# Weight transfers of 512 KB into six half-size buffers in a two-layer encoder kernel

## The chip, the cores and the metric

The kernel runs on one core of a Trainium2 chip. The metric is the device time of one execution in microseconds (us). Before the change the median of three runs is 2024.06 us (2023.92 to 2024.22).

## The reference, cut to what matters

The reference is two layers of an encoder over 256 tokens of width 2048, in float32:

```
h = RMSNorm(x);  [q | k | v | gu | gv] = h @ w_in
A = windowed attention on q, k, v (8 query heads, 2 key heads, a sink per head)
B = gelu(gu) * (W_s @ LayerNorm(gelu(gv)) + b_s)
x = x + concat(RMSNorm(A), RMSNorm(B)) @ w_o
x = x + (silu(g) * u) @ w_down,   [g | u] = DWConv3(RMSNorm(x) @ w_up)      # width 5632
```

Nearly all of the arithmetic is in the five products with weights. Each weight is read from memory once.

## The kernel before, in words

**Arithmetic.** TensorE (PE) multiplies in a reduced float32 form, so each operand is a sum of a rounded part, hi, and a rest, lo. A weight block is multiplied as hi against [hi | lo] of the activations (512 columns, L187 or L224), and as lo against the activations' hi (256 columns, L197 or L230). In the input projection of q, k, v and gv the activations stand still instead (L154 to L157). The products lo times lo are left out.

**How weights arrive.** `split_weights` takes 1024 KB of weights (128 partitions x 2048 numbers), which is eight blocks of 128 x 256. SP issues one transfer into a buffer called raw (L116; three buffers of 8 KB per partition). Then, for each half h of it (1024 numbers per partition), ScalarE (ACT) copies the half into a hi tile (L126) and VectorE (DVE) subtracts to get the lo tile (L108). There are four hi and four lo tiles. A raw buffer is free again when the lo of its second half is made; a lo tile is free again when the last lo matmul that reads it is done. The last transfer of a group of w_down holds four blocks, so 512 KB. In `pair`, which runs two weight columns of w_up together, the lo parts of the second column are made later (`split_later`).

**The order of work.** Each engine runs its instructions in a fixed order. That order is made at build time by a scheduler which places an instruction when its operands and buffers would be ready; code under `urgent()` gets a high priority, and `split_weights` is such code. The number, size and grouping of buffers therefore moves instructions of all engines, and the line order of the program doesn't tell where.

**The end of the first half of a layer.** The change and the prediction touch this stretch most. `gated(u)` computes a piece of gu (unit, L187 and L197), `spatial(u)` the product with W_s (L608), `gate(u)` multiplies both on DVE (L632) and adds its squares to a sum (ACT L276, DVE L277). There are four such pieces. `inv_rms_cols` then turns a sum of squares into 1/rms: DVE adds both halves of the sum (L289), PE sums over the partitions (L291), DVE scales (L281: `av` for attention, `sv` for gating), and GpSimd (POOL) takes the power (L283: `ar`, `sr`). `as_rows` spreads the result over partitions with two PE transposes (L298) and an ACT copy into rb (L300). `normed` then makes eight pairs of activation tiles for w_o: for each tile, DVE scales (L456), ACT makes hi (L254), DVE makes lo (L255).

**What covers the wait.** The product with w_o needs the attention half first. Three output columns are begun with it (`pre`, three units of L187 and L197 on attention tiles), and only then is each finished with the gating half:

```
663  pre = [unit(atts, w_o[l, u], None, 0, NK // 2, last=False) for u in range(3)]
666          ps = unit(mixT, w_o[l, u], pre[u], NK // 2, NK, first=False)
```

While PE works on `pre`, the chain from the last gate through L289, L291, L281, L283, L298, L300, L456, L254 has to be finished.

The product with w_up, `pair`, runs 32 hi matmuls of one column, 32 of the other, and then the 64 lo matmuls of both; it comes 21 times in each layer.

Of the kernel before, what the change touches and what calls it, by code (L numbers as in the profile page):

```python
# [8 lines left out]
F32 = mybir.dt.float32  # L9
# [5 lines left out]
P = 128  # L15
# [10 lines left out]
W = 512  # L26
KB = 4
# [13 lines left out]
def encoder(ctx: ExitStack, tc: tile.TileContext, xT, w_in, w_gu, w_o, w_up, w_down, wsT, pcol, prow, rope, out):  # L41
    nc = tc.nc
    pool = lambda name, bufs, **kw: ctx.enter_context(tc.tile_pool(name=name, bufs=bufs, **kw))
# [2 lines left out]
    slots = pool("slots", 42)  # L46
    rowp = pool("rowp", 4)
    evp = pool("evp", 4)
    rawp = pool("rawp", 3)
    hip = pool("hip", 4)  # L50
    lop = pool("lop", 4)
    scr = pool("scr", 4)
# [22 lines left out]
    def tp(shape):  # L75
        return tpp.tile(shape, F32, tag="tp", name="tp")

    xs = [const.tile([P, 2, SEQ], F32, tag=f"xs{j}", name=f"xs{j}") for j in range(NK // 2)]

    def urgent():  # L80
        return tc.high_priority(offset=AHEAD)


    def load_first(dst, src):
        tc.keep_in_program_order(nc.sync.dma_start(dst, src))
# [5 lines left out]
    with urgent():  # L91
        nc.vector.memset(ones, 1.0)

        warm = tp([P, P])
        for _ in range(WARM):
            nc.tensor.matmul(warm, ones, ones, start=True, stop=True)
        first_raws = [rawp.tile([P, 4 * W], F32, tag="raw", name="raw") for _ in range(2)]
        for k in range(KB):
            load_first(xs[k // 2][:, k % 2, :], xT[:, k, :])
            load_first(first_raws[0][:, k * W : (k + 1) * W], w_in[0, 2, :, k * W : (k + 1) * W])  # L100
        for k in range(KB):
            load_first(first_raws[1][:, k * W : (k + 1) * W], w_in[0, 0, :, k * W : (k + 1) * W])
    mhalf = const.tile([P, 8], F32, tag="mhalf", name="mhalf")
    nc.scalar.activation(mhalf, ones[:, :8], AF.Copy, scale=-0.5)

# [1 line left out]
    def lo_part(lo, part, hi):  # L107
        nc.vector.tensor_tensor(out=lo, in0=part, in1=hi.bitcast(F32), op=ALU.subtract)  # L108

    def split_weights(src, loaded=None, later=None):  # L110
        n = src.shape[-1]
        with urgent():
            raw = loaded
            if raw is None:
                raw = rawp.tile([P, 4 * W], F32, tag="raw", name="raw")
                nc.sync.dma_start(raw[:, :n], src)  # L116

            step = 2 * W if loaded is None else W
            his, los = [], []
            for h in range(0, n, 2 * W):  # L120
                hi = hip.tile([P, 2 * W], F32R, tag="hi", name="hi")
                lo = lop.tile([P, 2 * W], F32R, tag="lo", name="lo") if later is None else None
                for a in range(0, 2 * W, step):
                    part = raw[:, h + a : h + a + step]
                    cs = slice(a, a + step)
                    nc.scalar.activation(hi[:, cs], part, AF.Copy)  # L126
                    if later is None:
                        lo_part(lo[:, cs], part, hi[:, cs])
                    else:
                        later.append((part, hi[:, cs]))  # L130
                his.append(hi)
                los.append(lo)
        return his, los
# [12 lines left out]
    def rows_by_cols(ps, acts, src, first, last, raw=None):  # L146
        his, los = split_weights(src, raw)
        for kk in range(KB):
            cs = slice(kk % 2 * W, (kk % 2 + 1) * W)
            wh, wl = his[kk // 2][:, cs], los[kk // 2][:, cs]  # L150
            ms = [slice(m * P, (m + 1) * P) for m in range(2)]
            s0, s1 = first and kk == 0, last and kk == KB - 1
            for m in range(2):
                nc.tensor.matmul(ps[:, m, :], acts[kk][:, 0, ms[m]], wh, start=s0, stop=False)  # L154
                nc.tensor.matmul(ps[:, m, :], acts[kk][:, 1, ms[m]], wh, start=False, stop=False)  # L155
            for m in range(2):
                nc.tensor.matmul(ps[:, m, :], acts[kk][:, 0, ms[m]], wl, start=False, stop=s1)  # L157
# [5 lines left out]
    def unit(acts, w, ps=None, k0=0, k1=None, first=True, last=True):  # L163
# [3 lines left out]
        for g in range(k0, k1, 2 * UB):  # L167
            ks = range(g, min(g + 2 * UB, k1))
            his, los = [], []
            for b in range(g, ks.stop, UB):  # L170
                h, lo = split_weights(w[:, b * UW : min(b + UB, ks.stop) * UW])
                his += h
                los += lo
# [38 lines left out]
    def pair(acts, ws):  # L212
        pss, his, los, later = [mm(), mm()], [], [], []
        for n, w in enumerate(ws):
            hs = []
            for b in range(0, len(acts), UB):
                h, lo = split_weights(w[:, b * UW : (b + UB) * UW], later=later if n else None)
                hs += h
                los += lo if n == 0 else []
            for k in range(len(acts)):  # L220
                for i in range(2):
                    c = k % KB * UW + i * P
                    x1 = acts[k].rearrange("p a b -> p (a b)")
                    nc.tensor.matmul(pss[n][:, i, :], hs[k // KB][:, c : c + P], x1, start=k == 0, stop=False)  # L224
        for n in range(2):
            los = split_later(later) if n else los
            for k in range(len(acts)):
                for i in range(2):
                    c = k % KB * UW + i * P
                    nc.tensor.matmul(  # L230
                        pss[n][:, i, :SEQ], los[k // KB][:, c : c + P], acts[k][:, 0, :], start=False, stop=k == len(acts) - 1
                    )
        after_lo[0] = True
        return pss
# [111 lines left out]
    def rotate(rows, m, nh, tab):  # L346
        v = rows.rearrange("p (h d) -> p h d", d=HD)
        a = sl([P, nh, HD])
        nc.vector.tensor_tensor(
            out=a, in0=v, in1=tab[:, 0, m, :].unsqueeze(1).to_broadcast([P, nh, HD]), op=ALU.mult  # L350
        )
        b = sl([P, nh, HD])
        for lo, hi in ((0, 64), (64, 0)):
            nc.vector.tensor_tensor(
                out=b[:, :, lo : lo + 64],
                in0=v[:, :, hi : hi + 64],
                in1=tab[:, 1, m, lo : lo + 64].unsqueeze(1).to_broadcast([P, nh, 64]),
                op=ALU.mult,
            )
        nc.vector.tensor_tensor(out=a, in0=a, in1=b, op=ALU.add)  # L360
        return a
# [137 lines left out]
    for l in range(DEPTH):  # L499
# [38 lines left out]
        for m in range(2):  # L538
            a = rotate(kv[m][:, : 2 * HD], m, 2, tabs[1])
# [148 lines left out]
        for f0, f1 in ((0, 24), (24, NF)):  # L688
# [21 lines left out]
            for u in range(8):  # L710
                ps = [tp([P, W]) for _ in range(2)] if last and not more and u == 7 else mm()
                unit(ys, w_down[l, u, :, f0 * UW : f1 * UW], ps)
                if last and not more:
                    for i in range(2):
                        part = ps[i] if isinstance(ps, list) else ps[:, i, :]
# [64 lines left out]
```

## Time and profile before

| | |
|---|---|
| median of 3 runs | 2024.06 us |
| the profiled execution's own time | 2021.3 us |
| its span, first to last instruction | 2019.5 us |
| granted TensorE clock, mean | 1.000 |
| DVE busy | 1407.3 us (70%) |
| ACT busy | 1057.9 us (52%) |
| share of the 16 DMA engines taken by queue q1 (weights) | 53.6% |
| instructions of PE (matmuls) | 11324 |

A row of the timeline gives the start, the length, the engine, the line and operation, the tile written and the tiles read, the shape, and how many equal instructions in sequence it stands for; in square brackets stands the idle time before it and what ended that. The length of a PE row runs to the modelled end of its last matmul, so the rate of matmuls is read from start to start.

### The profile page before, as it was taken

The page shows a single profiled execution, that of the slowest core. Times are in us where ns is not written, and L with a number is a line of the kernel's source. Part 1 is how long each engine was busy: PE and PEld are TensorE (multiplying, and loading weights), DVE is VectorE, ACT ScalarE, POOL GpSimd, SP SyncE. Part 2 cuts the span into 40 slices and gives each one's busy share as a digit, 9 for nine tenths or more (in the row PEclk, how much of TensorE's full clock was granted, in tenths as well). Part 3 has the DMA queues.
Part 4 walks back from the last instruction along what each step waited for, and adds up shares of the span by engine and source line. Part 5 has one row for each costly group of instructions (what it writes and reads, how often), then busy time and mean ns, then how long its engine had stood idle before and what let it go on. Part 6 is the DMA issues. An engine that isn't in the chain of part 4 may idle for free.

```text
span 2019.5 us, 28222 instructions
## 1 busy us (share of the span) xinstructions
PE 2009.2 (99%) x11324; PEld 1761.7 (87%) x11324; DVE 1407.3 (70%) x1969; ACT 1057.9 (52%) x1429; POOL 20.7 (1%) x25
## 2 busy tenths in 40 slices
PE   9999999999999999999999999999999999999999
PEld 7888888898888888888888888889888888888888
DVE  6869767777755577777667797667777555777754
ACT  6575545555533355555445655555555334555542
POOL 0000000000000000000000000000000000000000
PEclk9999999999999999999999999999999999999999
DMA  8644555455555554555565345545555554455564
GB/s 292 224 148 150 179 175 203 171 174 213 197 188 188 189 186 167 204 201 189 182 245 183 130 167 171 205 167 175 210 199 202 190 188 171 167 205 210 177 212 136
DMA packets 59891, 380.25 MB, mean 188 GB/s; under 512 B 6896, under 2 KB 9968, under 8 KB 15984
## 3 DMA queue, kind: packets, MB, share of 16 engines
q1 hardware_dynamic: 59616, 378.43, 53.6%
q8 instruction: 88, 1.44, 0.3%
q14 instruction: 43, 0.35, 0.1%
q10 hardware_dynamic: 144, 0.02, 0.0%
HBM read 376.33 MB, written 2.10 MB: 187 GB/s over the span
## 4 chain that ended last, share of the span: by engine, by line
PE 98%; DVE 1%; POOL 0%; DMA 0%; ACT 0%; SPq 0%; issue 0%; DVEq 0%
PE mm L224 30%; PE mm L187 25%; PE mm L230 16%; PE mm L197 13%; PE mm L154 3%; PE mm L157 3%; PE mm L155 3%; PE tp L187 0%; PE tp L266 0%; PE tp L608 0%; PE tp L267 0%; PE tp L268 0%; PE tp L436 0%; DMA raw<-in_w_in 0%; PE tp L197 0%; DVE sl L261 0%
## 5 line engine op out<-in xcount | busy, mean ns | idle before, releaser
L108 DVE TENSOR_TENSOR lo<-raw,hi 128x1024 fp32r<-128x1024 f32 (+1 forms) x708 | 831.4, 1214 | 414.2 <-issue 137.8
L126 ACT ACTIVATE hi<-raw 128x1024 fp32r<-128x1024 f32 (+1 forms) x708 | 731.1, 1051 | 700.0 <-PE mm L187 319.2
L224 PE MATMUL mm<-sl,hi 128*128 128x512 f32 x2688 | 617.4, 389 | 0.0
L224 PEld LDWEIGHTS mm<-sl,hi 128*128 128x128 f32 x2688 | 501.9, 188 | 102.7
L187 PE MATMUL mm<-sl,hi 128*128 128x512 f32 x2264 | 529.4, 390 | 0.0
L187 PEld LDWEIGHTS mm<-sl,hi 128*128 128x128 f32 x2264 | 419.9, 188 | 83.6
L230 PEld LDWEIGHTS mm<-sl,lo 128*128 128x128 f32 x2688 | 328.1, 192 | 3.3
L230 PE MATMUL mm<-sl,lo 128*128 128x256 f32 x2688 | 329.1, 283 | 0.0
L197 PEld LDWEIGHTS mm<-sl,lo 128*128 128x128 f32 x2264 | 282.2, 191 | 7.6 <-ACT sl L254 1.9
L197 PE MATMUL mm<-sl,lo 128*128 128x256 f32 x2264 | 287.5, 284 | 0.0
L680 DVE SCALAR_TENSOR_TENSOR sc<-ev,pc,sc 128x255 f32<-128x255 f32 x176 | 81.0, 482 | 105.5 <-ACT sc L679 105.5
L154 PE MATMUL mm<-hi,sl 128*128 128x512 f32 x320 | 126.2, 394 | 0.1
L155 PE MATMUL mm<-hi,sl 128*128 128x512 f32 x320 | 125.2, 391 | 0.0
L239 ACT COPY ev<-mm 128x512 f32<-128x512 f32 x96 | 55.6, 579 | 129.5 <-PE mm L230 114.3
L157 PE MATMUL mm<-lo,sl 128*128 128x512 f32 x320 | 99.8, 391 | 0.0
L679 ACT ACTIVATE sc<-ev,pc 128x256 f32<-128x256 f32 x176 | 98.7, 586 | 0.0
L683 DVE SCALAR_TENSOR_TENSOR sc<-ev,pc,sc 128x255 f32<-128x255 f32 x176 | 80.9, 482 | 3.0
L154 PEld LDWEIGHTS mm<-hi,sl 128*128 128x128 f32 x320 | 60.3, 188 | 12.6 <-ACT hi L126 0.6
L155 PEld LDWEIGHTS mm<-hi,sl 128*128 128x128 f32 x320 | 60.1, 188 | 11.6
L157 PEld LDWEIGHTS mm<-lo,sl 128*128 128x128 f32 x320 | 59.7, 188 | 12.0
L254 ACT ACTIVATE sl<-sl 128x256 fp32r<-128x256 f32 x88 | 32.1, 409 | 71.3 <-DVE sl L701 71.3
L241 DVE TENSOR_TENSOR ev<-mm,ev 128x512 f32<-128x512 f32 x96 | 65.6, 684 | 0.0
(124 smaller groups left out, 787.9 us busy)
## 6 DMA issues: line engine op xcount, KB each, us to landing
raw<-in_w_up SPq DMA_DIRECT2D x176, 1024.0 KB, 6.0
raw<-in_w_down SPq DMA_DIRECT2D x80, 1024.0 KB, 5.1
raw<-in_w_in SPq DMA_DIRECT2D x38, 1024.0 KB, 5.0
raw<-in_w_o SPq DMA_DIRECT2D x32, 1024.0 KB, 5.1
raw<-in_w_gu SPq DMA_DIRECT2D x16, 1024.0 KB, 5.1
raw<-in_w_down SPq DMA_DIRECT2D x16, 512.0 KB, 3.6
sl<-in_prow SPq DMA_DIRECT2D x12, 256.0 KB, 6.1
raw<-in_w_in SPq DMA_DIRECT2D x8, 256.0 KB, 5.3
```

Source lines behind the costliest of these rows:

```text
L108: nc.vector.tensor_tensor(out=lo, in0=part, in1=hi.bitcast(F32), op=ALU.subtract)
L126: nc.scalar.activation(hi[:, cs], part, AF.Copy)
L154: nc.tensor.matmul(ps[:, m, :], acts[kk][:, 0, ms[m]], wh, start=s0, stop=False)
L155: nc.tensor.matmul(ps[:, m, :], acts[kk][:, 1, ms[m]], wh, start=False, stop=False)
L157: nc.tensor.matmul(ps[:, m, :], acts[kk][:, 0, ms[m]], wl, start=False, stop=s1)
L187: nc.tensor.matmul(bank[i], tile_of(his, k, i), x1, start=begins and k == k0, stop=flipped and tail and k == k1 - 1,)
L197: nc.tensor.matmul(bank[i][:, :SEQ], tile_of(los, k, i), acts[k][:, 0, :], start=False, stop=not flipped and tail and k == k1 - 1,)
L224: nc.tensor.matmul(pss[n][:, i, :], hs[k // KB][:, c : c + P], x1, start=k == 0, stop=False)
L230: nc.tensor.matmul(pss[n][:, i, :SEQ], los[k // KB][:, c : c + P], acts[k][:, 0, :], start=False, stop=k == len(acts) - 1)
L679: nc.scalar.activation(t[:, i, :], s[:, i, :], AF.Identity, bias=col(3), scale=col(1))
L680: nc.vector.scalar_tensor_tensor(out=t[:, i, 1:], in0=s[:, i, : SEQ - 1], scalar=col(0), in1=t[:, i, 1:], op0=ALU.mult, op1=ALU.add)
L683: nc.vector.scalar_tensor_tensor(out=t[:, i, : SEQ - 1], in0=s[:, i, 1:], scalar=col(2), in1=t[:, i, : SEQ - 1], op0=ALU.mult, op1=ALU.add)
```

## The change

The raw buffers become six of half the size, and the transfer moves into the loop over halves. So each half of 512 KB has its own buffer, its own transfer, its own hi and its own lo. The two transfers at the start of the program that come in pieces of 256 KB keep these pieces, but lie in two half buffers each. `split_weights` had 342 transfers of 1024 KB and now issues 684 of 512 KB for them; the 16 of 512 KB stay. The lines after L100 move: line 116 is line 119 now, and from the hi copy on each line is one higher (L126 is L127, L187 is L188, L291 is L292), while L108 keeps its number.

```diff
-    rawp = pool("rawp", 3)
+    rawp = pool("rawp", 6)
...
-        first_raws = [rawp.tile([P, 4 * W], F32, tag="raw", name="raw") for _ in range(2)]
-        for k in range(KB):
-            load_first(xs[k // 2][:, k % 2, :], xT[:, k, :])
-            load_first(first_raws[0][:, k * W : (k + 1) * W], w_in[0, 2, :, k * W : (k + 1) * W])
-        for k in range(KB):
-            load_first(first_raws[1][:, k * W : (k + 1) * W], w_in[0, 0, :, k * W : (k + 1) * W])
+        first_raws = [[rawp.tile([P, 2 * W], F32, tag="raw", name="raw") for _ in range(2)] for _ in range(2)]
+        for c, raws in zip((2, 0), first_raws):
+            for k in range(KB):
+                if c == 2:
+                    load_first(xs[k // 2][:, k % 2, :], xT[:, k, :])
+                load_first(raws[k // 2][:, k % 2 * W : (k % 2 + 1) * W], w_in[0, c, :, k * W : (k + 1) * W])
...
-            raw = loaded
-            if raw is None:
-                raw = rawp.tile([P, 4 * W], F32, tag="raw", name="raw")
-                nc.sync.dma_start(raw[:, :n], src)
 
             step = 2 * W if loaded is None else W
             his, los = [], []
             for h in range(0, n, 2 * W):
+                if loaded is None:
+                    raw = rawp.tile([P, 2 * W], F32, tag="raw", name="raw")
+                    nc.sync.dma_start(raw, src[:, h : h + 2 * W])
+                else:
+                    raw = loaded[h // (2 * W)]
...
-                    part = raw[:, h + a : h + a + step]
+                    part = raw[:, a : a + step]
```

The work of PE and DVE is the same, instruction for instruction; ACT has two more loads of its function table in layer 0. What moves is the order. In the feed-forward half of a layer the orders of PE agree but for small exchanges. In layer 0's attention two more halves are split ahead, and this shifts what follows.

PE in layer 0, at the sum of squares of the gating half. `tp_1863` is the sum over partitions, `sr_1869` its inverse root, `mm_2002` the third column of `pre`, whose hi matmuls are going on. Before:

```order
L187 MATMUL mm_2002<-sl_1522,hi_2009 128x512 x2
L187 MATMUL mm_2002<-sl_1527,hi_2009 128x512 x2
L291 MATMUL tp_1863<-ones_101,sl_1382 128x1 [waits DVE_49]
L291 MATMUL tp_1863<-ones_101,sl_1382 128x1
L187 MATMUL mm_2002<-sl_1532,hi_2009 128x512 x2
L298 MATMUL tp_1871<-ident_130,sr_1869 128x128 [waits Pool_49]
L298 MATMUL tp_1871<-ident_130,sr_1869 128x128
L187 MATMUL mm_2002<-sl_1537,hi_2009 128x512 x2
L197 MATMUL mm_2002<-sl_1502,lo_2006 128x256 x2
L197 MATMUL mm_2002<-sl_1507,lo_2006 128x256 x2
L197 MATMUL mm_2002<-sl_1512,lo_2006 128x256 x2
```

The same place after the change; `mm_2060` is the third column of `pre`, `sl_1932` to `sl_1967` are the tiles of the gating half:

```order
L198 MATMUL mm_2060<-sl_1559,lo_2064 128x256 x2
L198 MATMUL mm_2060<-sl_1564,lo_2070 128x256 [waits DVE_49]
L198 MATMUL mm_2060<-sl_1564,lo_2070 128x256
L198 MATMUL mm_2060<-sl_1569,lo_2070 128x256 x2
L198 MATMUL mm_2060<-sl_1574,lo_2070 128x256 x2
L198 MATMUL mm_2060<-sl_1579,lo_2070 128x256 x2
L292 MATMUL tp_1917<-ones_101,sl_1420 128x1 [waits DVE_49,PE_49]
L292 MATMUL tp_1917<-ones_101,sl_1420 128x1
L299 MATMUL tp_1925<-ident_132,sr_1923 128x128 [waits PE_49,Pool_49]
L299 MATMUL tp_1925<-ident_132,sr_1923 128x128
L198 MATMUL mm_1970<-sl_1932,lo_2108 128x256 [waits Activation_49]
...
L198 MATMUL mm_1970<-sl_1937,lo_2108 128x256 [waits Activation_49]
```

Four L187 of the third column and its 16 L197 stood behind L291 and around L298; now all of the third column stands ahead of L292, and the next matmul after the transposes reads a tile of the gating half.

DVE at the same place, up to the scaling `sv`. `sl_1382` is the sum of squares, a `lo` named here is for w_o, `sc_1859` the last piece of squares. Before:

```order
L277 TENSOR_TENSOR sl_1382<-sl_1382,sc_1763 128x512 [waits Activation_49]
L108 TENSOR_TENSOR lo_2048<-raw_2045,hi_2047 128x1024 [waits DMAHW6_49,PE_49]
L277 TENSOR_TENSOR sl_1382<-sl_1382,sc_1859 128x512 [waits DVE_49,Activation_49]
L108 TENSOR_TENSOR lo_2052<-raw_2045,hi_2051 128x1024 [waits PE_49]
L289 TENSOR_TENSOR sl_1382<-sl_1382 128x256 [waits DVE_49]
L281 TENSOR_SCALAR sv_1867<-tp_1863 128x2 [waits PE_49]
```

After; `sl_1420` is the sum, and with four lo tiles `lo_2161` takes the place of `lo_2064` and `lo_2167` that of `lo_2070`, the two that PE reads just ahead of L292:

```order
L108 TENSOR_TENSOR lo_2161<-raw_2158,hi_2160 128x1024 [waits DMAHW5_49,PE_49]
L278 TENSOR_TENSOR sl_1420<-sl_1420,sc_1813 128x512 [waits Activation_49]
L108 TENSOR_TENSOR lo_2167<-raw_2164,hi_2166 128x1024 [waits DMAHW6_49,PE_49]
L278 TENSOR_TENSOR sl_1420<-sl_1420,sc_1913 128x512 [waits DVE_49,Activation_49]
L290 TENSOR_TENSOR sl_1420<-sl_1420 128x256 [waits DVE_49]
L282 TENSOR_SCALAR sv_1921<-tp_1917 128x2 [waits PE_49]
```

Both additions to the sum now stand behind a lo that waits for PE. Before, `lo_2048` and `lo_2052` took the places of the lo tiles of the second column of `pre`, a whole run of hi matmuls earlier on PE.

ACT after the copy into rb, in the program after the change, where the tiles of the gating half get their hi (before, all eight stood in a row with no weight copy between them):

```order
L301 COPY rb_1928<-tp_1925 128x256 [waits PE_49]
L255 ACTIVATE sl_1932<-sc_1930 128x256 [waits DVE_49]
L255 ACTIVATE sl_1937<-sc_1935 128x256 [waits DVE_49]
L255 ACTIVATE sl_1942<-sc_1940 128x256 [waits DVE_49]
L255 ACTIVATE sl_1947<-sc_1945 128x256 [waits DVE_49]
L255 ACTIVATE sl_1952<-sc_1950 128x256 [waits DVE_49]
L255 ACTIVATE sl_1957<-sc_1955 128x256 [waits DVE_49]
L127 ACTIVATE hi_2215<-raw_2213 128x1024 [waits DMAHW7_49,PE_49,Activation_49]
L255 ACTIVATE sl_1962<-sc_1960 128x256 [waits DVE_49]
```

A hi copy, which itself waits for PE, has moved in ahead of the seventh tile.

## Rows read from the trace of the kernel before

**Rows 1.** The page, busy time by engine and the chain that ended last

```profile
PE 2009.2 (99%) x11324; PEld 1761.7 (87%) x11324; DVE 1407.3 (70%) x1969; ACT 1057.9 (52%) x1429; POOL 20.7 (1%) x25
PE 98%; DVE 1%; POOL 0%; DMA 0%; ACT 0%; SPq 0%; issue 0%; DVEq 0%
```

**Rows 2.** Waits of PE over the span: us in total, times, longest

```profile
PE tp L551 <- DVE sl L540: 1.0, 1, 1.0
PE tp L298 <- POOL sr L283: 0.9, 2, 0.4
PE tp L266 <- DVE sl L261: 0.6, 2, 0.4
PE tp L298 <- POOL ar L283: 0.5, 1, 0.5
```

**Rows 3.** Busy time by stretch, one in the feed-forward of layer 0

```profile
300.00:1000.00 700.00, 699.99 (x4032) 619.82 (x4032) 482.83 (x631) 360.21 (x470) 0.00 (x0) 1.00 0.54 190
```

**Rows 4.** Timeline of the feed-forward stage, one `pair` and the next

```profile
500.39 14.70 PE L224 MATMUL mm<-sl,hi 128*128 128x512 f32 x64
...
501.67 2.01 ACT L126 ACTIVATE hi<-raw 128x1024 fp32r<-128x1024 f32 x2 [0.49 <-DMA raw<-in_w_up]
...
514.92 7.83 PE L230 MATMUL mm<-sl,lo 128*128 128x256 f32 x64
...
522.59 14.70 PE L224 MATMUL mm<-sl,hi 128*128 128x512 f32 x64
```

**Rows 5.** Waits of SP over the span: us in total, times, longest

```profile
SPq L116 <- DVE lo L108: 1774.9, 346, 15.1
```

**Rows 6.** The page, weights' queue (packets, MB, share) and DMA issues (KB, us)

```profile
q1 hardware_dynamic: 59616, 378.43, 53.6%
...
raw<-in_w_up SPq DMA_DIRECT2D x176, 1024.0 KB, 6.0
...
raw<-in_w_down SPq DMA_DIRECT2D x16, 512.0 KB, 3.6
```

**Rows 7.** Timeline, DVE ahead of the gating sum in layer 0

```profile
197.45 1.22 DVE L108 TENSOR_TENSOR lo<-raw,hi 128x1024 fp32r<-128x1024 f32 x1
...
198.59 0.69 DVE L277 TENSOR_TENSOR sl<-sl,sc 128x512 f32<-128x512 f32 x1
...
199.19 1.22 DVE L108 TENSOR_TENSOR lo<-raw,hi 128x1024 fp32r<-128x1024 f32 x1
...
200.33 0.41 DVE L289 TENSOR_TENSOR sl<-sl 128x256 f32<-128x256 f32 x1
```

**Rows 8.** Timeline, from the gating sum to the first gating tiles

```profile
200.86 0.55 PE L291 MATMUL tp<-ones,sl 128*128 128x1 f32 x4
...
202.43 0.43 PE L298 MATMUL tp<-ident,sr 128*128 128x128 f32 x2 [0.45 <-POOL sr L283]
...
202.62 0.71 PE L187 MATMUL mm<-sl,hi 128*128 128x512 f32 x2
202.90 0.37 ACT L300 COPY rb<-tp 128x256 f32<-128x256 f32 x1 [1.64 <-PE tp L298]
...
203.31 1.67 DVE L456 SCALAR_TENSOR_TENSOR sc<-sl,pc,rb 128x256 f32<-128x256 f32 x4 [1.71 <-ACT rb L300]
...
204.39 1.32 ACT L254 ACTIVATE sl<-sc 128x256 fp32r<-128x256 f32 x4
204.90 1.43 DVE L255 TENSOR_TENSOR sl<-sc,sl 128x256 fp32r<-128x256 f32 x4
```

**Rows 9.** Timeline, where PE has caught up again

```profile
209.82 3.36 PE L187 MATMUL mm<-sl,hi 128*128 128x512 f32 x14
```

**Rows 10.** Timeline, the attention sum in layer 0

```profile
168.84 0.50 PE L291 MATMUL tp<-ones,sl 128*128 128x1 f32 x4
169.20 1.07 PE L197 MATMUL mm<-sl,lo 128*128 128x256 f32 x7
...
170.37 0.43 PE L298 MATMUL tp<-ident,ar 128*128 128x128 f32 x2
```

## The prediction, on record before the changed kernel ran

> **What bounds the kernel now.** I read the page first: PE is busy 99% of the span and the chain that ended last is PE for 98% of it [rows 1]. Busy time of pipelined matmuls overlaps, so I looked for idle time of PE next, in the list of its waits. The feed-forward stage has none: between 300 and 1000 us PE is busy for 699.99 of 700 us [rows 3]. What there is lies in the attention halves: L551 1.0 us once, the transposes L298 0.9 and 0.5 us, L266 0.6 us [rows 2]. So a change to the weights' path gains at most those 3.0 us (wherever it shortens them), and it loses whatever new wait it puts on PE.
>
> PE's pace comes from start to start in the timeline: 514.92 - 500.39 = 14.53 us for 64 hi matmuls, 227 ns each, and 522.59 - 514.92 = 7.67 us for 64 lo matmuls, 120 ns each [rows 4].
>
> **The change part by part: the transfers.** 342 transfers become 684 of half the size. In the trace a transfer of 1024 KB lands in 6.0 us, one of 512 KB in 3.6 us [rows 6]. Two halves one after another would take 7.2 us, but several are in flight, and the weights' queue takes 53.6% of the 16 DMA engines [rows 6]. SP spends 1774.9 us waiting for DVE's lo, that is, for a free buffer [rows 5]: it has the time for 342 more issues, and is held by buffers and not by the transfers. In the `pair` stage the third hi tile (it and the fourth are copied from 501.67 on, 2.01 us for two) is done near 502.7, and PE needs it after 16 matmuls, at 500.39 + 16 x 0.227 = 504.0 [rows 4]. That is 1.3 us of cover. Half buffers come free one by one as each lo is made, so the copies can start earlier than now. I cost the feed-forward at 0: no stall is there to be removed, and no transfer comes later. If the cover went, each 0.1 us would be paid 42 times, 4.2 us; I use that as a rival.
>
> The Trainium skill speaks against the change here: "DMA: Bandwidth & Descriptors", Bandwidth, asks for transfers of 1 MiB or more to reach three quarters of the peak rate. By that rule the smaller transfers would run at a lower rate. The trace agrees as to direction (1024 KB in 6.0 us is 175 GB/s for a lone transfer, 512 KB in 3.6 us is 146 GB/s) [rows 6], but the queue is not what PE waits for. By the rule alone the sum would be that of the third rival below; by the rows it is 0.
>
> **The order: gating sum, DVE in front of it (term A).** PE in layer 0 arrives at the sum L292 with nothing left of `pre`. The last thing before it is eight L198 on `lo_2070`, eight before these on `lo_2064`. DVE must make `lo_2161` in the place of `lo_2064`, so it starts it only once the first of these two runs of eight is done; call that moment 0. In DVE's order then follow `lo_2161`, L278, `lo_2167`, L278, L290, and L292 needs the last. The prices, start to start, from the same kinds of rows: lo 1.14 (198.59 - 197.45, and 200.33 - 199.19), L278 0.60 (199.19 - 198.59), L290 0.41 [rows 7]. Sum 1.14 + 0.60 + 1.14 + 0.60 + 0.41 = 3.89, plus about 0.1 from PE to DVE (an estimate from the other hops here) and 0.12 back to PE (200.33 + 0.41 = 200.74 to 200.86 [rows 7, 8]): 4.1 us. PE has 8 x 0.120 = 0.96 us of work in it. A = +3.15. Before, the same DVE work ran under twelve L187 and PE came to L291 without a wait. Bounds: at least +1.0, if only `lo_2167` stood in the way and the rest were done (1.14 + 0.60 + 0.41 + 0.2, less what overlaps); at most +4, if DVE comes late to `lo_2161`.
>
> **Sum to transposes (term B).** From L291 to L298 it takes 202.43 - 200.86 = 1.57 us, through DVE and POOL [rows 8]. Before, two L187 (0.45 us) were run in it; after, none stand between. The 1.57 us remain: B = +0.45, which is close to sure.
>
> **Transposes to the first gating tiles (term C).** Before, 2 L187 and 24 L197 of cover stood behind L298 [rows 8], and from 202.62 until 209.82 [rows 9] PE got 13 L187 and 32 L197 done, 13 x 0.227 + 32 x 0.120 = 6.79 us of work in 7.20: a loss of 0.41 us. After, the next matmul needs the first gating tile's hi. With T the start of L299: rb starts at T + 0.47 (202.90 - 202.43) and is done 0.37 later; L457 takes 0.40 per tile start to start and 0.48 for the first (4 in 1.67 us), L255 0.33 (4 in 1.32) and an estimated 0.41 for one alone, L256 0.35 (4 in 1.43) [rows 8]. First hi: T + 0.88 + 0.48 + 0.04 + 0.41 = T + 1.81, first matmul T + 1.9, where PE could have gone on at T + 0.2 (202.62 - 202.43): 1.7 us. Following the tiles through the three engines in their new order costs another 0.6 us between the first and the sixth (each is ready 0.1 to 0.2 us after PE asks for it). Between the sixth and the seventh stands `hi_2215`, about 1.0 us on ACT (2 in 2.01 [rows 4]), which waits for a matmul only 1 us ahead of where PE then is: 0.7 us. Sum 3.0, less the 0.41 lost there now: C = +2.6. Bounds +1.3 (only the first tile, less the present loss) and +3.5.
>
> **The attention sum (term D).** Before, seven L197 ran between L291 and L298 (168.84 to 170.37, 1.53 us) [rows 10], 0.84 us of cover. After, two L188 do, 0.45 us. D = +0.39. L290 is just in time for L292 there by the same prices (DVE's chain of lo tiles ends within 0.1 us of PE's matmuls), so up to +0.7 is possible.
>
> **The rest.** The keys' turn L551 waits 1.0 us now [rows 2]; after, DVE has one small step less in front: E = -0.2, between 0 and -1.0. Two half tiles are split further ahead in layer 0's attention, and the second head group is interleaved with another unit: cost 0, bounds -1 and +1. Two more table loads on ACT lie beside PE work there. Layer 1 has L292 and L299 with the same matmuls around them as before, and the feed-forward the same order: 0.
>
> Sum: 3.15 + 0.45 + 2.6 + 0.39 - 0.2 = +6.4 us. The profiled execution took 2021.3 us (span 2019.5), so 2027.7. The median of the runs shown is 2024.06, 2.8 above the profiled one, and the forecast stands in its terms: 2024.06 + 6.4 = 2030.4, or 0.31% more. A measurement of this kernel tells 0.2%, 4.05 us, from no change.
>
> **The rivals.** First, the stall is smaller: PE loses time further up (DVE and ACT are close behind it in the attention half), so that moment 0 comes later for both and PE meets less of the chain, or the shifted order saves some of the 3.0 us of present waits. With A at 1.0 to 1.5, C at 1.3 and the rest of the terms as above or 1 us better: +1 to +4, 2025 to 2028, within 0.2%. For it: the present waits are there; against: A hangs on a named wait (`lo_2161` on the last L198 of `lo_2064`) that no earlier delay removes.
>
> Second, not slower: finer buffers take DVE's and ACT's lag away. The place is the attention half, where L551, L266 and the transposes wait 3.0 us now; the price is up to -3.0 us, and it decides if the halves split ahead leave DVE idle when PE reaches L292, so that A is 0 and C is covered. Then 2021 to 2024.5. Against it, the order has no cover behind L299 at all, which alone is B and most of C. A gain over 0.2% needs more than all present waits together.
>
> Third, the transfers become the bound in `pair`: the place is the third hi tile, with 1.3 us of cover. It decides once a half lands more than 1.3 us later than it does as part of a whole. Each 0.2 us beyond that is 42 x 0.2 = 8.4 us, together with the terms above +15: 2039. For it only the lone rate, 146 against 175 GB/s; against it SP's 1774.9 us of waiting for buffers [rows 5].
>
> **How the numbers follow.** Forecast, the chain at the gating sum stands: 0.57, with its own range +4 to +9 us, 2028 to 2033. Smaller stall: 0.32. Not slower: 0.06, of which 0.03 beyond 0.2%. Transfers: 0.05. The range of 8 in 10 takes the forecast's and most of the first rival's: 2025.5 to 2033. Faster by over 0.2%: 0.03. Within: 0.32 + 0.03 and the lower edge of the forecast's range, 0.37. Slower: 0.60.
>
> **What would show it.** In the profile after: a wait of PE at L292 for DVE L290 of about 3 us near 200 us, which the list of waits doesn't have now; the wait of L299 for POOL `sr` some 1.3 to 1.5 us in layer 0 and 0.4 in layer 1; the first L198 behind it waiting about 1.7 us for ACT L255; no wait of PE between 300 and 1000 us. The forecast is wrong if L292 shows no wait, if PE waits for a hi tile or a transfer in `pair`, or if layer 1 or the feed-forward differ by over 1 us.

## The result, and the profile after

The changed kernel takes 2031.76 us (median of 5, 2030.3 to 2033.79) against 2024.06 (median of 5): 7.7 us more. The ratio is 1.0040, with a 95% interval of 1.0028 to 1.0051. The forecast was 2030.4 with 2025.5 to 2033. Run again beside three of the experiments, it took 2032.18 against 2023.09, a ratio of 1.0041 (1.0028 to 1.0053).

The profiled execution took 2033.79 us (span 2031.9); it is the slowest of the five, and that of before, 2021.3, lies below the median of its runs. So the two profiles lie 12.4 us apart, which is 4.7 us more than the medians, and the place of each term is read from more than one profile below.

The page of the changed kernel, for [rows 1, 6]:

```profile
PE 2014.9 (99%) x11324; PEld 1764.5 (87%) x11324; DVE 1418.0 (70%) x1969; ACT 1063.7 (52%) x1431; POOL 20.9 (1%) x25
...
q1 hardware_dynamic: 108864, 378.45, 55.3%
...
PE 97%; DVE 1%; POOL 0%; issue 0%; DMA 0%; ACT 0%; SPq 0%; DVEq 0%; ACTq 0%
...
raw<-in_w_up SPq DMA_DIRECT2D x352, 512.0 KB, 5.4
```

The same number of matmuls, and a weights' queue that is hardly busier: 55.3% against 53.6%.

The waits of PE (total, times, longest), for [rows 2]:

```profile
PE tp L292 <- DVE sl L290: 3.3, 1, 3.3
PE tp L299 <- POOL xr L284: 2.1, 2, 1.6
PE mm L198 <- ACT sl L255: 2.0, 2, 1.4
PE tp L299 <- POOL sr L284: 1.5, 2, 1.0
...
PE tp L552 <- DVE sl L541: 1.0, 1, 1.0
PE tp L299 <- POOL ar L284: 0.9, 2, 0.5
```

The first and the third are new, and the fourth has grown from 0.9. One wait is smaller than before: L267 (L266 then) waits 0.2 us in all, where it waited 0.6 [rows 2]. [rows 2] leaves out two lines of the list of before: L96 at the start of the program, 1.1 us, and the longest of all,

```profile
PE tp L298 <- POOL xr L283: 2.1, 2, 1.6
```

It is unchanged here (second line above); e8 below is about it. The place of the new waits is the gating sum in layer 0; its timeline, for [rows 7 to 9]:

```profile
204.22 2.07 PE L198 MATMUL mm<-sl,lo 128*128 128x256 f32 x16
...
205.38 1.22 DVE L108 TENSOR_TENSOR lo<-raw,hi 128x1024 fp32r<-128x1024 f32 x1
...
206.52 0.68 DVE L278 TENSOR_TENSOR sl<-sl,sc 128x512 f32<-128x512 f32 x1
207.12 1.22 DVE L108 TENSOR_TENSOR lo<-raw,hi 128x1024 fp32r<-128x1024 f32 x1
208.26 0.69 DVE L278 TENSOR_TENSOR sl<-sl,sc 128x512 f32<-128x512 f32 x1
208.98 0.42 DVE L290 TENSOR_TENSOR sl<-sl 128x256 f32<-128x256 f32 x1
...
209.55 0.98 PE L292 MATMUL tp<-ones,sl 128*128 128x1 f32 x4 [3.26 <-DVE sl L290]
...
211.56 0.69 PE L299 MATMUL tp<-ident,sr 128*128 128x128 f32 x2 [1.03 <-POOL sr L284]
...
213.68 1.65 PE L198 MATMUL mm<-sl,lo 128*128 128x256 f32 x6 [1.43 <-ACT sl L255]
...
219.94 1.06 ACT L127 ACTIVATE hi<-raw 128x1024 fp32r<-128x1024 f32 x1 [3.33 <-PE mm L188]
...
221.35 0.81 PE L198 MATMUL mm<-sl,lo 128*128 128x256 f32 x4 [0.58 <-ACT sl L255]
222.00 1.31 PE L188 MATMUL mm<-sl,hi 128*128 128x512 f32 x5
```

One sees the chain lo, L278, lo, L278, L290 on DVE, without a gap, and PE idle behind its 16 L198. The loss of the whole site (this stretch of PE, from the third column to the gating tiles) is worked out so. PE has done its third column at 204.22 + 16 x 0.120 = 206.14, and is past the eighth gating tile at 222.00: 15.86 us. In them it did 16 L198, 12 L188, four parts of L292 and two of L299, which at full pace is 16 x 0.120 + 12 x 0.227 + 0.66 = 5.30 us (0.66 is the start to start of the six small ones). Loss 10.56 us. Before, the second column's lo run began at

```profile
196.20 2.08 PE L197 MATMUL mm<-sl,lo 128*128 128x256 f32 x16
```

and by the same count, with 48 L197 and 27 L187 until 209.82 [rows 9], the loss was 13.62 - (48 x 0.120 + 27 x 0.227 + 0.66) = 1.07 us.

The granted clock (last but two) in stretches of the changed kernel (PE, PEld, DVE, ACT, POOL busy; clock; DMA share; GB/s):

```profile
43.00:45.00 2.00, 2.00 (x6) 1.58 (x5) 0.00 (x0) 0.00 (x0) 0.00 (x0) 0.50 0.51 195
195.00:200.00 5.00, 5.00 (x41) 4.82 (x40) 4.91 (x9) 2.85 (x5) 0.00 (x0) 1.00 0.31 87
205.00:210.00 5.00, 1.74 (x14) 1.57 (x13) 4.37 (x6) 1.57 (x3) 0.00 (x0) 0.93 0.82 248
210.00:215.00 5.00, 2.54 (x11) 2.06 (x12) 2.47 (x8) 1.58 (x4) 0.70 (x1) 0.50 0.31 100
215.00:220.00 5.00, 5.00 (x18) 4.24 (x18) 2.96 (x8) 1.27 (x4) 0.00 (x0) 0.55 0.00 0
220.00:230.00 10.00, 9.42 (x57) 8.14 (x56) 6.18 (x9) 6.01 (x9) 0.00 (x0) 1.00 0.36 107
300.00:1000.00 700.00, 699.95 (x4032) 619.67 (x4031) 486.28 (x629) 361.73 (x469) 0.70 (x1) 1.00 0.55 190
```

This the prediction did not have: the clock falls to the lower of its two levels, 0.50 (1.2 of 2.4 GHz), after PE has stood idle, and stays there for some 10 us while matmuls run again. The first row is another such place, behind the wait for `xr`. Before, it was 1.00 throughout. The last row is the feed-forward stage, 699.95 of 700 us busy, as in [rows 3].

### The profile page after: what moved, and what is told of

Its sections match the earlier page's. It is cut to its first block, busy times and chain, and to the rows that moved or that the text cites. A ratio compares the mean times of both kernels' runs of the same rounds, so it can differ in the third digit from the quotient of the medians.

```text
span 2031.9 us, 29271 instructions
## 1 busy us (share of the span) xinstructions
PE 2014.9 (99%) x11324; PEld 1764.5 (87%) x11324; DVE 1418.0 (70%) x1969; ACT 1063.7 (52%) x1431; POOL 20.9 (1%) x25
## 3 DMA queue, kind: packets, MB, share of 16 engines
q1 hardware_dynamic: 108864, 378.45, 55.3%
## 4 chain that ended last, share of the span: by engine, by line
PE 97%; DVE 1%; POOL 0%; issue 0%; DMA 0%; ACT 0%; SPq 0%; DVEq 0%; ACTq 0%
PE mm L225 30%; PE mm L188 25%; PE mm L231 16%; PE mm L198 13%; PE mm L155 3%; PE mm L156 3%; PE mm L158 3%; DVE lo L108 0%; PE tp L188 0%; PE tp L267 0%; PE tp L609 0%; PE tp L268 0%; PE tp L269 0%; PE tp L437 0%; DMA raw<-in_w_in 0%
## 5 line engine op out<-in xcount | busy, mean ns | idle before, releaser
L127 ACT ACTIVATE hi<-raw 128x1024 fp32r<-128x1024 f32 (+1 forms) x708 | 745.7, 1054 | 830.4 <-PE mm L188 349.8
L108 DVE TENSOR_TENSOR lo<-raw,hi 128x1024 fp32r<-128x1024 f32 (+1 forms) x708 | 830.9, 1214 | 462.0 <-PE mm L231 146.5
L188 PE MATMUL mm<-sl,hi 128*128 128x512 f32 x2264 | 532.2, 391 | 0.0
L188 PEld LDWEIGHTS mm<-sl,hi 128*128 128x128 f32 x2264 | 420.7, 189 | 83.7
L198 PEld LDWEIGHTS mm<-sl,lo 128*128 128x128 f32 x2264 | 283.4, 192 | 10.7 <-ACT sl L255 5.2
L198 PE MATMUL mm<-sl,lo 128*128 128x256 f32 x2264 | 288.8, 284 | 2.1 <-ACT sl L255 2.0
L681 DVE SCALAR_TENSOR_TENSOR sc<-ev,pc,sc 128x255 f32<-128x255 f32 x176 | 84.7, 481 | 8.3 <-ACT sc L680 5.2
L684 DVE SCALAR_TENSOR_TENSOR sc<-ev,pc,sc 128x255 f32<-128x255 f32 x176 | 85.2, 484 | 6.1
L497 DVE TENSOR_TENSOR xs<-mm,xs 128x512 f32<-128x512 f32 x80 | 54.9, 686 | 8.4 <-PE mm L188 8.0
```

Source lines behind the costliest of these rows:

```text
L188: nc.tensor.matmul(bank[i], tile_of(his, k, i), x1, start=begins and k == k0, stop=flipped and tail and k == k1 - 1,)
L198: nc.tensor.matmul(bank[i][:, :SEQ], tile_of(los, k, i), acts[k][:, 0, :], start=False, stop=not flipped and tail and k == k1 - 1,)
L681: nc.vector.scalar_tensor_tensor(out=t[:, i, 1:], in0=s[:, i, : SEQ - 1], scalar=col(0), in1=t[:, i, 1:], op0=ALU.mult, op1=ALU.add)
L684: nc.vector.scalar_tensor_tensor(out=t[:, i, : SEQ - 1], in0=s[:, i, 1:], scalar=col(2), in1=t[:, i, : SEQ - 1], op0=ALU.mult, op1=ALU.add)
```

## The experiments

The order theory: the time is lost where the scheduler's new order has PE arrive at the gating sum with nothing left to do, as idle time and as slow matmuls behind it. Its rival: smaller transfers or finer buffers cost by themselves.

**e1, five half buffers.**

```diff
-    rawp = pool("rawp", 6)
+    rawp = pool("rawp", 5)
```

> The changed kernel with five half buffers and not six: same 512 KB transfers, but in layer 0 the order of PE and DVE around the gating sum stands as before the change (four hi and 16 lo matmuls of the third column behind the sum). Order theory (the time is lost in the new order at the gating sum, partly as idle time, partly as matmuls at the low granted clock behind it): within 2 us of the kernel before; wait at the sum none, L299 on sr about 0.4 us, granted clock 1.00 from 195 to 230 us. Transfer rival (smaller transfers or finer buffers cost by themselves): still 5 to 8 us over the kernel before.

Measured: 2026.73 us against 2023.15, ratio 1.0015 (1.0006 to 1.0024), so 3 us over, and some 5 under the changed kernel. With this one number changed the site is whole again: no wait at the sum, L299 on `sr` 0.9 us in both layers together, clock 1.00. By the count above, from the second column's lo run at 197.03 to 210.66, its loss is 1.08 us, as before the change. (No run puts back PE's order alone and keeps six half buffers.) But the time missed the order theory's 2 us. Its waits of PE:

```profile
PE tp L267 <- DVE sl L262: 2.3, 4, 1.1
PE mm L198 <- ACT sl L255: 2.1, 4, 0.9
...
PE mm L198 <- DVE lo L108: 0.8, 1, 0.8
```

The order has moved elsewhere too: the turn of the attention probabilities (L267) waits 2.3 us where it waited 0.6 [rows 2], and the first unit of w_down waits for its last activation tiles or a lo, up to 0.9 us at a time and 2.9 us in all. The 3 us that are left are so seen in the profile, but whether the size of the transfers or the order causes them isn't told apart here.

**e2, the size at the old buffers.**

```diff
-                nc.sync.dma_start(raw[:, :n], src)
+                for h in range(0, n, 2 * W):
+                    nc.sync.dma_start(raw[:, h : h + 2 * W], src[:, h : h + 2 * W])
```

> The kernel before with its three buffers of 8 KB, each filled by two transfers of 512 KB: the size of a transfer alone. Order theory: within 1.5 us of the kernel before, with the same waits. Transfer rival: 5 to 8 us over the kernel before, or at least half of that, with waits of PE for hi tiles in the feed-forward stage.

Measured: 2024.57 against 2023.15, ratio 1.0009 (1.0000 to 1.0017), so 0 to 3.4 us. The waits of PE are those of before [rows 2], and one besides:

```profile
PE mm L198 <- ACT sl L255: 2.4, 3, 0.9
```

That is the start of w_down, three of four times; so the expectation held for the time and not for "the same waits". No wait for a transfer or for a hi tile is in the list. But the edit doesn't change the size alone: the scheduler moves instructions of ACT and DVE here too, and at this very place. In the kernel before, a hi copy (916.10) stands on ACT between the last two activation tiles (915.77 and 917.04); in e2 both tiles stand in a row (916.06) and the hi copy behind them. So 0 to 3.4 us, by the interval, is the price of the size and of that order together.

**e5, the changed kernel again**, for a second profile.

> The changed kernel once more, beside the next three kernels. All theories: 7 to 9 us over the kernel before; the same waits at the gating sum (L292 3.3 us, L299 1.0, L198 1.4), and the low granted clock between 210 and 220 us again if it belongs to the site and not to one run.

Measured: 2032.18 us (above). The same site, with the low clock for a shorter time (0.80 between 205 and 210 us, 0.52 between 210 and 215, 1.00 after):

```profile
PE mm L198 <- ACT sl L255: 3.9, 5, 1.4
...
207.40 0.58 PE L292 MATMUL tp<-ones,sl 128*128 128x1 f32 x4 [3.25 <-DVE sl L290]
...
209.00 0.69 PE L299 MATMUL tp<-ident,sr 128*128 128x128 f32 x2 [1.03 <-POOL sr L284]
...
211.12 1.65 PE L198 MATMUL mm<-sl,lo 128*128 128x256 f32 x6 [1.43 <-ACT sl L255]
...
212.57 2.33 PE L188 MATMUL mm<-sl,hi 128*128 128x512 f32 x5
...
217.83 0.82 PE L198 MATMUL mm<-sl,lo 128*128 128x256 f32 x4 [0.59 <-ACT sl L255]
218.49 2.68 PE L188 MATMUL mm<-sl,hi 128*128 128x512 f32 x11
```

The third column was done at 203.99 (14 L198 left at 202.31), so the site's loss is 218.49 - 203.99 - 5.30 = 9.20 us here. Five L188 take 2.33 us at the low clock, where five took 1.31 at the high one (222.00 above). Of the first line, 2.0 us are the two waits at this site; the other three, 0.31, 0.72 and 0.86 us (568.56, 1573.03 and 1929.83), are at the start of w_down.

**e3 and e6, DVE's order.** Both hold the two lo tiles back on DVE (`held` is the instruction that they are queued behind); e3 behind L290, e6 behind the scaling sv.

```diff
+        with tc.issue_after(held[0]) if held[0] is not None else ExitStack():
             nc.vector.tensor_tensor(out=lo, in0=part, in1=hi.bitcast(F32), op=ALU.subtract)
...
+                held[0] = summed[-1].ins if l == 0 and u == 1 else None
                 ps = unit(mixT, w_o[l, u], pre[u], NK // 2, NK, first=False)
```

> The changed kernel, in which DVE makes the two lo tiles of the second output column in layer 0 behind the addition L290 (L295 here) and not ahead of the two additions to the sum. PE's order is that of the changed kernel. Order theory: the wait at the sum falls from 3.3 to about 1.5 us (the two additions and L290 remain, some 1.6 us, behind ACT's last square), the rest of the site stays; 2 us under the changed kernel if the clock still falls, 4 to 6 us if it doesn't. Transfer rival: no change beyond 1 us.

> The changed kernel, in which DVE makes the two lo tiles behind the scaling sv (L282, here L287) and so ahead of nothing that PE waits for there; behind L290 alone (e3) the first of them stood before sv and the wait only moved on to L299. Order theory: the wait at the sum about 1.9 us as in e3, L299 on sr back at 1.0 us, first gating tile as in the changed kernel or up to 0.6 us later: 1 to 1.5 us less idle time, and 1 to 3 us under the changed kernel. Rival (the time at this site is set by the clock alone): no difference beyond 1 us.

Measured: e3 2031.72 (ratio 1.0041, 1.0029 to 1.0054), e6 2032.21 (1.0042, 1.0029 to 1.0054): nothing gained, and both expectations missed. The wait at the sum did fall, to 1.9 us in both. So 1.4 of the 3.3 us were the two lo tiles; 1.9 us remain from the last gate itself, whose squares (ACT) and additions end that late. In e3 one lo then stood between L290 and sv, the other just ahead of POOL's power, which took 1.61 us, and L299's wait grew to 2.2 us. In e6 both stood behind sv, and this is its timeline:

```profile
206.85 0.58 PE L299 MATMUL tp<-ones,sl 128*128 128x1 f32 x4 [1.88 <-DVE sl L297]
207.47 0.16 DVE L287 TENSOR_SCALAR sv<-tp 128x2 f32<-128x2 f32 x1 [0.76 <-PE tp L299]
207.55 1.22 DVE L111 TENSOR_TENSOR lo<-raw,hi 128x1024 fp32r<-128x1024 f32 x1
207.71 1.61 POOL L291 TENSOR_TENSOR sr<-sv,mhalf 128x2 f32<-128x2 f32 x1 [28.46 <-DVE sv L287]
...
209.37 0.69 PE L306 MATMUL tp<-ident,sr 128*128 128x128 f32 x2 [1.94 <-POOL sr L291]
```

POOL's power took 1.61 us and not 0.70, and ended 0.55 us after DVE's lo. So most of the 1.4 us won at the sum was lost at the next link, in both. A place for the lo tiles behind POOL's power was not tried.

**e4, e7 and e9, the clock.** Matmuls on old data are put into PE's gaps, so that the clock stays up (results unused).

```diff
+            with tc.issue_after(last.ins):
+                for _ in range(JUNK):
+                    d = nc.tensor.matmul(t[:, SEQ:], x[:, 0, :P], x[:, 0, :], start=True, stop=True)
```

> The changed kernel with 24 matmuls of 256 columns on old data put into PE's idle time ahead of the gating sum in layer 0 (their results are not used). 24 x 0.120 = 2.9 us of the 3.3 us wait are so filled. Order theory with a clock share: the sum starts as late as in the changed kernel, but the granted clock stays at 1.00 where it was 0.50 to 0.55 between 210 and 220 us; the matmuls behind it run at 227 and 120 ns, so 3 to 4 us under the changed kernel. If the clock has no part: no change within 1 us.

> As e4, with 10 more matmuls on old data between the sum and its transposes and 12 behind the transposes, so that all three gaps at the site are filled (24, 10 and 12 of 120 ns in 3.3, 1.0 and 1.4 us). If the low clock comes from PE's idle time: granted clock 1.00 from 195 to 230 us, the matmuls of the first gating tiles at 227 and 120 ns, and 2 to 4 us under the changed kernel, since the filling itself costs next to nothing. If the clock falls all the same, or falls and costs nothing: within 1 us of the changed kernel.

> As e7, but the 12 matmuls behind the transposes write into the PSUM tile of the sum and not into that of the transposes, so that the copy into rb need not wait for them (in e7 it started 1.84 us after the transposes, in the changed kernel 0.73). The granted clock stays at 1.00, so from the start of the transposes to the seventh gating tile's first matmul it should take 7.3 us, by the terms of the prediction, where the changed kernel took 8.8 at the low clock: 1.4 to 1.6 us under the changed kernel. If the clock costs nothing here: within 0.5 us of it.

Measured: e4 2032.02 (1.0046, 1.0033 to 1.0060), e7 2032.04 (1.0041, 1.0029 to 1.0054), e9 2031.01 against 2023.04 (1.0040, 1.0026 to 1.0054). In e4 the clock fell all the same, at 213 us, behind the two gaps that were left (1.0 and 1.4 us). In e7 it stayed at 1.00, but the filling itself was in the way: the copy into rb waited for the last of it.

```profile
208.95 0.38 PE L316 MATMUL tp<-ident,sr 128*128 128x128 f32 x2
...
210.79 0.37 ACT L322 COPY rb<-tp 128x256 f32<-128x256 f32 x1 [6.46 <-PE tp L320]
```

In e9, with that mended, clock and site:

```profile
205.00:210.00 5.00, 4.71 (x40) 4.51 (x39) 2.56 (x5) 0.35 (x1) 0.70 (x1) 1.00 0.69 234
210.00:215.00 5.00, 4.99 (x31) 4.27 (x30) 4.95 (x14) 2.48 (x8) 0.00 (x0) 1.00 0.02 7
215.00:220.00 5.00, 4.43 (x22) 3.42 (x21) 2.22 (x4) 2.59 (x4) 0.00 (x0) 1.00 0.30 97
```

```profile
204.16 3.04 PE L300 MATMUL tp<-sl 128*128 128x256 f32 x24
...
209.23 0.38 PE L318 MATMUL tp<-ident,sr 128*128 128x128 f32 x2
...
211.04 0.90 PE L202 MATMUL mm<-sl,lo 128*128 128x256 f32 x4
...
216.38 0.81 PE L202 MATMUL mm<-sl,lo 128*128 128x256 f32 x4 [0.57 <-ACT sl L259]
217.03 4.25 PE L192 MATMUL mm<-sl,hi 128*128 128x512 f32 x18
```

From the transposes to the seventh tile it takes 216.38 - 209.23 = 7.15 us, where the changed kernel took 217.83 - 209.00 = 8.83 (e5). The site's loss, the filling counted in, is 217.03 - 204.16 - 5.30 = 7.57 us against 9.20. So the low clock costs 1.6 us here and the idle chain 7.57 - 1.07 = 6.5 us. That is read from one profile of each. The times don't show it: the medians are 1.1 us apart and both spread by 2 to 4 us, and the ratios, 1.0040 and 1.0041, are the same within their intervals.

**e8, a version that beats both.** The largest wait that before and after share is that of the transposes for `xr` (L298 before, 1.6 us in layer 0 and 0.5 in layer 1). In the kernel before, its transposes are queued behind the key columns:

```diff
-                r1b = as_rows(r1)
-            in_rows(psk, 2, b)
+            last = in_rows(psk, 2, b)
+            if b == NB - 1:
+                with tc.issue_after(last.ins):
+                    r1b = as_rows(r1)
             in_rows(psq, 0, b)
```

> The kernel before, with the transposes for xr (L298, both layers) queued behind the last matmul of the key columns instead of two matmuls behind the sum; rb is needed much later. The 1.6 and 0.5 us that PE waits there now should go, since the power on POOL then runs under 14 matmuls: 1.8 to 2.4 us under the kernel before, and up to 1.6 more in runs in which the granted clock falls at that wait. If what PE waits for is only late elsewhere then: no change within 1 us.

Measured: 2019.65 us against 2023.09, ratio 0.9982 (0.9973 to 0.9991): 3.4 us faster than before and 12.5 faster than the changed kernel. Its largest waits:

```profile
PE tp L96 <- DVE ones L92: 1.1, 1, 1.1
PE tp L554 <- DVE sl L543: 1.0, 1, 1.0
```

The wait for `xr` (2.1 us) is gone, and nothing took its place. The rest, 1.3 us, fits the clock: the 15 runs of before beside it spread from 2021.1 to 2026.2, and the four slowest had a mean clock of 0.999; the 11 of e8 lie within 2.1 us, all at 1.000. In one profile of the changed kernel the clock was 0.50 from 43 to 45 us, right behind the same 1.6 us wait, and in e5's it was 1.00 there. That the spread of before comes from this site was not profiled run by run, and stays likely.

**e10, e1 and e8 together.** Both edits above.

> e1 and e8 in one: five half buffers, and the transposes for xr behind the key columns. If the two effects add: e1's 3 us over the kernel before less e8's 3.4 us, so within 1.5 us of the kernel before. If finer buffers gain once the wait at xr is gone: 2 us or more under it, as e8.

Measured: 2024.54 against 2023.04, ratio 1.0006 (0.9997 to 1.0014). The two effects add, a little on the slow side (3.0 less 3.4 would be -0.4 us, and it is +1.2): finer buffers gain nothing with the wait at `xr` gone.

## Why the prediction was right, step by step

**What bounds.** Held in the main: PE is busy 99% of the span, and the new time is new waits of PE. In the profile of the changed kernel PE has no wait between 300 and 1000 us, but e5's has one of 0.31 us (568.56, w_down). The "3.0 us" of present waits were a wrong reading: the list of before adds up to 6.2 us, with the 2.1 for `xr` as its largest line. The forecast doesn't hang on it, but the rival "not slower" had too low a bound, and e8 gained 3.4 us, more than "all present waits together".

**The transfers, costed at 0.** Held in `pair`: a half lands in 5.4 us, SP waits for buffers, and PE waits there for no transfer and no hi tile. (At the program's start it waits 0.8 us for a hi copy, at 9.00 in the first profile and not in e5's.) The prediction's 175 and 146 GB/s are not rates of lone transfers: its rows are medians over transfers that run beside others. The rule of the Trainium skill on transfers of 1 MiB ("DMA: Bandwidth & Descriptors", Bandwidth) was set against this. By the rule a half would move at a lower rate; in flight with others it did take nearly as long as a whole (5.4 and 6.0 us), which agrees, and PE in `pair` didn't wait for it. What the cost of 0 left out is the start of w_down, where PE waits up to 0.9 us for the last activation tiles: 2.4 us of such waits in e2's profile, 1.9 in e5's, and 0.3 to 2.9 in the other profiles with 512 KB transfers (e1's 2.9 with a wait for a lo in it) but the first of the changed kernel, which has none. The two profiles with 1024 KB (before, e8) have none. So this is a likely cost of the change, by size or by order. In e5's profile it is more than the 1 us by which the prediction would have called itself wrong in the feed-forward. Whether some executions of before have such waits too is open.

**Term A, 3.15 us.** Measured 3.25 and 3.26, with the predicted chain on DVE, gapless. The prediction hung it all on the two lo tiles; e3 shows that 1.9 us of it stay without them, since the last gate's product (L633) ran on DVE until the first lo could start, and its squares come later still. So the chain was right, and that its two causes ended together was luck.

**Term B, 1.57 us from sum to transposes.** 1.60 in e5 (207.40 to 209.00). In the first profile 2.01, since the clock was down already at L292.

**Term C, 1.9 us to the first gating tile's matmul and, with the 12 L198 and 12 L188 between and the 0.6 and 0.7 us of the prediction, 7.4 to the seventh's.** With the clock held up (e9): 1.81 and 7.15. The hi copy between the sixth and the seventh tile showed as predicted (219.94 in the profile after, 0.58 us of idle time behind it).

**Terms D and E.** L299 on `ar` waits 0.9 us over both layers where it was 0.5: +0.4, as D had it. L552 waits its 1.0 us as before: E's -0.2 didn't come.

**What was missing.** A term for the clock. The prediction added idle times and took the matmuls behind them at 227 and 120 ns; in the gap the clock fell, and they ran at half speed: 1.6 us in e5, some 3 in the first profile. The sum then is 6.5 (A to C, predicted 3.15 + 0.45 + 2.6 = 6.2), 0.4 (D) and 1.6 (clock), 8.5 us in all, against 7.7 and 9.1 measured in the two series. With the 1.9 us at w_down, 10.4 of the 10.8 us between the spans of e5 (2030.3) and of before (2019.5) have a place. The medians lie closer together than these two profiles because executions of before are mostly slower than the one that was profiled. So the number stayed inside the range partly because the range reached 2.6 us over the sum; the terms for the clock and w_down were at nothing. The Trainium skill says that TensorE's clock is halved when the engine has not been busy ("TensorE: Matmul & The Clock Gate", Part 1); the rows agree as to the two levels, and with that sentence in mind the term could have been named.

**The rivals.** A smaller stall: no, A was there in full. Not slower: no, 0.4 us of present waits was saved (L266, from 0.6 to 0.2) and nothing else. Transfers in `pair`: no wait there.

## What to carry to other kernels

A change of buffers under a scheduler is a change of order: read where each engine's queue stands at the few places where a long chain must be covered, and price the chain link by link from rows; here transfers of 512 KB cost PE nothing in `pair`, and an order that left PE without work at the gating sum cost 6.5 us. Idle time on TensorE had a tail here, the lower clock (1.6 us in e5), and it likely makes equal runs unequal (e8). Read the whole list of waits before bounding a gain: the largest one was passed over. To remove a wait, it helped here to queue PE's waiting instruction behind work that was ready (e8); moving DVE's part of the chain did not help (e3, e6).

## What the runs showed of the hardware

POOL's power on 256 numbers takes 0.70 us alone (210.81 in the changed kernel, `sr`) and 1.61 to 1.77 us when DVE starts a lo subtraction of 1.22 us just ahead of it (e3 and e6, and `xr` of layer 0 in every profile). In the kernel before that lo runs from 39.53 to 40.76:

```profile
39.56 1.77 POOL L283 TENSOR_TENSOR xr<-xv,mhalf 128x2 f32<-128x2 f32 x1 [37.33 <-ACT hi L126]
```

It ends about 0.55 us after DVE each time, as if it had waited DVE out and were not merely slowed. The Trainium skill gives this as a rule ("SBUF — State Buffer", Who interferes with whom): of a DVE instruction with two inputs in SBUF and a GpSimd instruction that reads SBUF, the one that comes second is blocked until the first has ended. The rows agree where POOL comes second. They don't show the other half: in layer 1 of the kernel before, the lo starts 0.05 us behind the power (1045.29 and 1045.24), and both take their usual time, 1.23 and 0.70 us.

The granted clock doesn't fall each time after the same wait. Behind the 1.6 us of idle PE at `xr` it was 0.50 in two profiles (the changed kernel's and e4) and 1.00 in the other eight that have this wait. Behind the gaps at the gating sum it fell in all five profiles in which two gaps of 1.0 us or more were left (the changed kernel, e3 to e6), and neither in e7, where one of 1.4 us was left, nor in e9, where the longest was 0.6 us.
